# Opening of a transformer trunk written anew: modulation weights loaded ahead of tokens, their products as columns, tokens turned in pairs

## Chip, cores and metric

The kernel runs on one core of one Trainium2 chip. The time is the device time of an execution in microseconds (us); the profile shows one profiled execution with its own span.

## What is computed

A trunk of two layers over 1024 tokens of width 1024. Each layer scales and shifts an RMS norm by six vectors that come from the condition `c` through a matrix `w_mod`, projects it into three groups of attention heads (A, B, C), joins their outputs, and then does the same with a gated feed-forward part. The part that the change touches is the very first one, in layer 0:

```python
cond = jax.nn.silu(c)
mod = cond @ w_mod[l] + b_mod[l]                  # (1, 6 * 1024)
sh_a, sc_a, gt_a, sh_f, sc_f, gt_f = split_cols(mod, (D,) * 6)
h = rms_norm(x, g_attn[l]) * (1 + sc_a) + sh_a    # the opening computes this for l = 0
proj = h @ w_in[l]                                # ... and the first parts of this
```

All data are 32-bit. A value is kept as a high and a low part, so that a product takes three fast matmuls (high x high, low x high, high x low).

## The kernel before

TensorE is `pe`, ScalarE `act`, VectorE `dve`, GpSimd `pool`; SyncE (`sp`) issues nearly all loads, in order. Within the opening (lines 723 to 861) the order on `pe`, `act`, `dve` and `sp` is pinned as written: each engine does its instructions in the order of the program text. Only what comes after line 861 is ordered by the scheduler.

**Data.** Tokens come in two halves of 512, each as four tiles of 128 tokens (`x_load`, 512 KB each, in `xn`). A tile is squared and summed on ScalarE (`x_square`; its output `junk` is thrown away, the sum goes into a column of `rx`). `x_rms` takes the root and VectorE the reciprocal; `spread` turns these four columns into rows (`ps_r`, copied to `rb`). `x_turn` transposes the tokens on TensorE, four 128x128 blocks to a PSUM bank (`ps_x`), and copies them into `xt`, which holds the width on its partitions: block n of `xt` is the n-th 128 of the width.

**Modulation.** Only the shift and scale of the first norm are needed at once, 2048 of the 6144 columns. They are made in four pairs p; pair p serves blocks 2p and 2p + 1. A pair has two pieces of `w_mod`, i = 2p and 2p + 1, one for each half of the rows; `gm_load(i)` loads one in two transfers of 512 KB into one of three buffers (`gm`). `gemv_half(i)` handles a piece: VectorE multiplies three of its four 128-row parts by the condition and sums them into `ga`; the fourth goes to TensorE. With the second piece TensorE sums `ga` over its partitions (`ones`). In the kernel before this gives a row of 512 values in PSUM (`ps_mod`), which ScalarE copies (`gr`) and four small transposes bring onto partitions (`gemv_turn`, `ps_m`). `gemv_finish(p)` adds the bias and makes the scale `gsc`. The vectors for that (bias and gains, `v72`) are loaded by GpSimd and transposed by `turn_vecs`.

**The norm's output.** `h_blocks(half, rows, ns)` makes blocks of h: `nt` on VectorE (tokens x scale x rows), then the high part `hh` on ScalarE, then the low part `hl` on VectorE.

**First products.** `c_first(n)` multiplies block n with the first weights of group C for four token tiles into four PSUM banks (`pssC`): 12 matmuls of 512 columns. These weights come as four tiles of 512 KB (`wc_stage`), split in two parts by `w_high` (ScalarE) and the function that it returns (VectorE, `wlo`). `a_first(u, p)` does two of eight row blocks of one early tile of the A projection (`pssA`, two banks): 6 matmuls. Its weights (`a_stage`, `a_high`) lie in parts of `hh` and `hl` that the second tokens fill later. Weight tiles (of C, of A, and `wab`) go through two buffers of the tag `wst`. `keep_busy` issues matmuls whose results are not used.

**After the opening** the loop over t (line 1056) starts with `c_proj(4, 5)`, the projection of token tiles 4 and 5, which takes h of the second half block by block. `spill` writes `xt` to memory in the meantime.

Of the kernel before, what the change touches and what calls it, by code (L numbers as in the profile page):

```python
# [85 lines left out]
def trunk(ctx: ExitStack, tc, A, C, out):  # L86
# [479 lines left out]
    def x_square(half, j, xn, r):  # L566
        junk = xt[:, 6:8, half * H : (half + 1) * H]
        act.activation(
            junk, xn.rearrange("p (a b) -> p a b", a=2), AF.Square, accum_out=r[:, j : j + 1]
        )  # L570
# [5 lines left out]
    def x_turn(half, xn, ns, engines):  # L576

        c = slice(half * H, (half + 1) * H)
        for n in ns:
# [7 lines left out]
            else:  # L587
                dve.tensor_copy(xt[:, n, c], ps)

# [25 lines left out]
    def gemv_half(i):  # L615
        p, s = i // 2, i % 2
        gm = gms.pop(i).rearrange("p k g n -> p k (g n)")
        if s == 0:
            gas[p] = stp.tile([P, 4 * P], F32, name="ga", tag="ga", bufs=2)
            gps[p] = psl.tile([P, 4 * P], F32, name="ps_mod", tag="mm")  # L620
        ga, row = gas[p], gps[p][0:1]
        for k in range(3):
            mod_add(4 * s + k, ga, gm[:, k])
        pe.matmul(row, condT[:, 4 * s + 3 : 4 * s + 4], gm[:, 3], start=(s == 0), stop=False)
        if s:
            pe.matmul(row, ones, ga, start=False, stop=True)
            gas[p] = stp.tile([1, 4 * P], F32, name="gr", tag="gr", bufs=1)
            act.copy(gas[p], row)

    def gemv_turn(p):  # L630

        ps = gps[p] = psl.tile([P, 4], F32, name="ps_m", tag="mm")
        row = gas.pop(p)
        for c in range(4):
            pe.transpose(ps[:, c : c + 1], row[:, c * P : (c + 1) * P], ident[0:1, 0:1])
# [14 lines left out]
    def h_blocks(half, rows, ns):  # L650
# [11 lines left out]
        for n, t in ts.items():  # L662
# [3 lines left out]
            )  # L666

# [6 lines left out]
    def c_first(n):  # L674

        wh, wl = wC[n // 2]
        for t in range(T0):
            ts_ = slice(t * P, (t + 1) * P)
            mm3(
                pssC[t], hh[:, n, ts_], hl[:, n, ts_], wh[:, n % 2], wl[:, n % 2],  # L680
                n == 0, n == KC - 1,
            )
# [42 lines left out]
    sp.dma_start(c8, A["c"][0].rearrange("(k p) -> k p", p=P))  # L725
    xns = [[x_load(0, j) for j in range(4)], []]
# [3 lines left out]
    gm_load(0)  # L730
    gm_load(1)
    wc_stage(0)
    a_stage(0)
    gm_load(2)
    rxs = [stp2.tile([P, 4], F32, name="rx", tag="rx", bufs=2) for _ in range(2)]
    act.activation(c8, c8, AF.Silu)
    idle = psl.tile([P, 4, P], F32, name="ps_idle", tag="mm")
# [5 lines left out]

    pst = psl.tile([P, 512], F32, name="pst", tag="mm")
    pe.transpose(pst[:, :KC], c8, ident[:KC, :KC])
    dve.tensor_copy(condT, pst[:, :KC])
    keep_busy(18)
    for j in range(4):
        x_square(0, j, xns[0][j], rxs[0])
    x_rms(rxs[0])  # L750
    x_turn(0, xns[0], range(KC), (act, act))
    gemv_half(0)
# [1794 lines left out]
```

## Time and profile before

| | us |
|---|---|
| median of 3 runs | 2385.76 |
| lowest and highest | 2385.19, 2387.93 |
| the profiled execution | 2386.03 |
| its span, first to last instruction | 2384.3 |

A row of the timeline has the start, the duration, the engine, the operation, the tile written and those read, the shape, how many instructions were merged into it, and in brackets the idle time before it and what ended that. A wide matmul is listed with about 0.39 us; matmuls are pipelined, so the next one starts sooner than that. PEld is the load of TensorE's weights. A group of instructions has count, busy time and mean time of one in ns, then the idle time before them.

### The profile page before, as it was taken

The page shows a single profiled execution, that of the slowest core. Times are in us where ns is not written, and L with a number is a line of the kernel's source. Part 1 is how long each engine was busy: PE and PEld are TensorE (multiplying, and loading weights), DVE is VectorE, ACT ScalarE, POOL GpSimd, SP SyncE. Part 2 cuts the span into 40 slices and gives each one's busy share as a digit, 9 for nine tenths or more (in the row PEclk, how much of TensorE's full clock was granted, in tenths as well). Part 3 has the DMA queues.
Part 4 walks back from the last instruction along what each step waited for, and adds up shares of the span by engine and source line. Part 5 has one row for each costly group of instructions (what it writes and reads, how often), then busy time and mean ns, then how long its engine had stood idle before and what let it go on. Part 6 is the DMA issues. An engine that isn't in the chain of part 4 may idle for free. (4 is left out here: it accounts for less than half of the span.)

```text
span 2384.3 us, 33350 instructions
## 1 busy us (share of the span) xinstructions
PE 2330.1 (98%) x11733; PEld 1949.5 (82%) x11733; DVE 1757.3 (74%) x2754; ACT 1186.5 (50%) x2264; POOL 781.9 (33%) x747
## 2 busy tenths in 40 slices
PE   8999999999999999999999999999999999999998
PEld 5788898888788888788888889988888888888886
DVE  5777898967957687586777689987796664537765
ACT  4422788944543333344533158897454333334443
POOL 1441356810244444200135124575015443430001
PEclk9999999999999999999999999999999999999999
DMA  8567417164345444586434861242633443329743
GB/s 279 150 194 227 138 28 198 34 210 126 111 143 175 131 154 153 183 259 186 155 96 132 256 186 28 72 120 74 225 102 126 153 155 103 104 98 297 214 121 111
DMA packets 307416, 358.00 MB, mean 150 GB/s; under 512 B 51996, under 2 KB 223868, under 8 KB 307248
## 3 DMA queue, kind: packets, MB, share of 16 engines
q1 hardware_dynamic: 290752, 346.26, 46.6%
q10 hardware_dynamic: 16128, 9.44, 1.5%
q8 instruction: 92, 1.51, 0.3%
q14 instruction: 76, 0.62, 0.1%
q0 software_dynamic: 368, 0.17, 0.0%
HBM read 270.84 MB, written 88.63 MB: 151 GB/s over the span
## 5 line engine op out<-in xcount | busy, mean ns | idle before, releaser
L49 PE MATMUL ps_d<-wpt 128*128 128x512 f32 x1848 | 423.8, 390 | 1.0 <-ACT wpt L49 0.7
L49 PEld LDWEIGHTS ps_d<-wpt 128*128 128x128 f32 x1848 | 345.7, 188 | 74.4 <-issue 3.0
L49 POOL TENSOR_SCALAR pr<-pr,rs 128x1024 f32<-128x1024 f32 (+2 forms) x248 | 190.2, 781 | 188.7 <-DVE rs L49 171.1
L49 POOL TENSOR_TENSOR sg<-sg,u 128x512 f32<-128x512 f32 x82 | 126.8, 1548 | 347.1 <-ACT sg L49 221.6
L49 PE MATMUL pv<-pt,vs 128*128 128x256 f32 x1088 | 176.1, 296 | 16.3 <-DVE y L49 13.7
L49 ACT CAST wpt<-w 128x512 fp32r<-128x512 f32 x154 | 95.7, 621 | 175.7 <-PE ps_d L49 155.0
L49 DVE TENSOR_TENSOR pt<-T,pt 128x512 fp32r<-128x512 f32 x272 | 177.6, 680 | 7.0 <-ACT pt L49 5.9
L49 ACT CAST pt<-T 128x512 fp32r<-128x512 f32 x272 | 151.7, 586 | 42.4 <-PE T L49 40.7
L49 ACT COPY u<-ps_w 128x512 f32<-128x512 f32 x128 | 75.1, 586 | 192.0 <-PE ps_w L49 187.1
L49 DVE SCALAR_TENSOR_TENSOR acc<-wmt,condT,acc 128x512 f32<-128x512 f32 (+1 forms) x98 | 117.0, 1202 | 71.5 <-DMA wmt<-in_w_mod_dram 70.7
L49 DVE TENSOR_TENSOR wpt<-w,wpt 128x512 fp32r<-128x512 f32 x154 | 109.1, 708 | 79.7 <-ACT wpt L49 75.4
L49 POOL TENSOR_TENSOR wpt<-ws,wpt 128x512 fp32r<-128x512 f32 x80 | 110.7, 1384 | 171.2 <-ACT wpt L49 132.4
L49 PEld LDWEIGHTS pv<-pt,vs 128*128 128x128 f32 x1088 | 142.2, 189 | 29.7 <-DVE y L49 25.4
L49 PE MATMUL T<-identr,pr 128*128 128x128 f32 x1176 | 160.8, 273 | 0.8 <-ACT edge L49 0.4
L49 PEld LDWEIGHTS T<-identr,pr 128*128 128x128 f32 x1176 | 137.8, 140 | 15.5 <-ACT edge L49 1.1
L49 ACT CAST wpt<-ws 128x512 fp32r<-128x512 f32 x176 | 107.8, 622 | 51.4 <-issue 22.9
L49 DVE TENSOR_TENSOR wpt<-graw,wpt 128x512 fp32r<-128x512 f32 x154 | 110.2, 716 | 17.3 <-ACT wpt L49 17.3
L49 ACT CAST wpt<-graw 128x512 fp32r<-128x512 f32 x154 | 95.0, 617 | 51.7 <-DMA graw<-gpd 43.3
L49 DVE TENSOR_REDUCE rs<-sC 128x1 f32<-128x1024 f32 x88 | 107.2, 1220 | 12.5 <-PE sC L49 11.4
L49 DVE TENSOR_TENSOR wlo<-wst,whi 128x1024 fp32r<-128x1024 f32 (+1 forms) x70 | 91.6, 1313 | 33.3 <-ACT whi L49 29.4
L49 DVE TENSOR_TENSOR wpt<-ws,wpt 128x512 fp32r<-128x512 f32 x96 | 81.0, 852 | 47.5 <-ACT wpt L49 47.2
L49 DVE TENSOR_TENSOR ws<-wr 128x512 f32<-128x512 f32 x88 | 81.3, 924 | 46.5 <-POOL wpt L49 43.0
(308 smaller groups left out, 5966.1 us busy)
## 6 DMA issues: line engine op xcount, KB each, us to landing
wr<-in_w_gu_dram SPq DMA_DIRECT2D x92, 512.0 KB, 4.1
gpd<-sg SPq DMA_DIRECT2D x154, 256.0 KB, 4.4
graw<-gpd SPq DMA_DIRECT2D x76, 512.0 KB, 3.8
w<-in_w_down_dram SPq DMA_DIRECT2D x110, 256.0 KB, 5.0
wmt<-in_w_mod_dram SPq DMA_DIRECT2D x48, 512.0 KB, 5.7
qk<-qkd SPq DMA_DIRECT2D x44, 512.0 KB, 7.0
wst<-in_w_o_dram SPq DMA_DIRECT2D x32, 512.0 KB, 4.2
wmt<-in_w_mod_dram SPq DMA_DIRECT2D x64, 256.0 KB, 3.9
```

What stands on the lines that cost most here:

```text
L49: ins = op(*args, **kwargs)
```

## The change

- Loads: the first two pieces of `w_mod` are issued ahead of the token tiles; the second weight tile of C goes ahead of piece 4, the two early A tiles and the second half's tokens go to other places in the queue.
- `gemv_half` makes columns: a 128x128 block of the piece (or of `ga`) is the weight, one column of the condition (or of ones) is streamed, and the four results stand in four columns of a bank. The sum of `ga` is a function that it returns, called later. `gemv_turn` and the copy `gr` are gone. For pair 1 (`kd=2`) VectorE does two of four parts and TensorE two.
- `x_turn_first` turns two token tiles at a time: one bank holds two blocks of the width for two tiles, and its copies are returned as functions, to be issued on VectorE or ScalarE at a chosen place. The second half still goes through `x_turn`, all copies on ScalarE.
- The root's table is asked for at the start. The vectors are turned after the first pair's columns. `rb` has two buffers; the first `h_blocks` reads the spread rows from PSUM.
- `c_first` runs its 12 matmuls by pass and not by token tile, and can do some passes alone; `h_blocks` can issue something between its low parts.
- The order of all calls is new: blocks 2 to 5 of `c_first` and the modulation pieces alternate; squares, turns and `h_blocks` of the second tokens come earlier among them, and the first step of the head norm (`first`) too.

```diff
--- before.py
+++ after.py
@@ -564,7 +564,7 @@
         return t
 
     def x_square(half, j, xn, r):
-        junk = xt[:, 6:8, half * H : (half + 1) * H]
+        junk = xt[:, 6:8, H:S]
         act.activation(
             junk, xn.rearrange("p (a b) -> p a b", a=2), AF.Square, accum_out=r[:, j : j + 1]
         )
@@ -587,6 +587,22 @@
             else:
                 dve.tensor_copy(xt[:, n, c], ps)
 
+    def x_turn_first(xn, pair, ms):
+
+        c = slice(pair * 2 * P, (pair + 1) * 2 * P)
+        copies = []
+        for m in ms:
+            ps = psl.tile([P, 2, 2 * P], F32, name="ps_x", tag="mm")
+            for a in range(2):
+                n = 2 * m + a
+                for i in range(2):
+                    pe.transpose(
+                        ps[:, a, i * P : (i + 1) * P],
+                        xn[2 * pair + i][:, n * P : (n + 1) * P], ident,
+                    )
+            copies.append(lambda copy, m=m, ps=ps: copy(xt[:, 2 * m : 2 * m + 2, c], ps))
+        return copies
+
     def load_vecs(l):
         v = stp.tile([72, P], F32, name="v72", tag="v72", bufs=2)
         pool.dma_start(v[0:48], A["b_mod"][l].rearrange("(k p) -> k p", p=P))
@@ -612,27 +628,27 @@
             rows = A["w_mod"][0, r0 : r0 + 4 * P, c0 : c0 + 2 * P]
             sp.dma_start(gm[:, :, g, :], rows.rearrange("(k p) n -> p k n", p=P))
 
-    def gemv_half(i):
+    def gemv_half(i, kd=3):
         p, s = i // 2, i % 2
         gm = gms.pop(i).rearrange("p k g n -> p k (g n)")
         if s == 0:
             gas[p] = stp.tile([P, 4 * P], F32, name="ga", tag="ga", bufs=2)
-            gps[p] = psl.tile([P, 4 * P], F32, name="ps_mod", tag="mm")
-        ga, row = gas[p], gps[p][0:1]
-        for k in range(3):
+            gps[p] = psl.tile([P, 4], F32, name="ps_m", tag="mm")
+        ga, ps = gas[p], gps[p]
+        for k in range(kd):
             mod_add(4 * s + k, ga, gm[:, k])
-        pe.matmul(row, condT[:, 4 * s + 3 : 4 * s + 4], gm[:, 3], start=(s == 0), stop=False)
+
+        def columns(src, col, start, stop):
+            for c in range(4):
+                pe.matmul(
+                    ps[:, c : c + 1], src[:, c * P : (c + 1) * P], col,
+                    start=start and c == 0, stop=stop, skip_group_check=True,
+                )
+
+        for k in range(kd, 4):
+            columns(gm[:, k], condT[:, 4 * s + k : 4 * s + k + 1], s == 0 and k == kd, False)
         if s:
-            pe.matmul(row, ones, ga, start=False, stop=True)
-            gas[p] = stp.tile([1, 4 * P], F32, name="gr", tag="gr", bufs=1)
-            act.copy(gas[p], row)
-
-    def gemv_turn(p):
-
-        ps = gps[p] = psl.tile([P, 4], F32, name="ps_m", tag="mm")
-        row = gas.pop(p)
-        for c in range(4):
-            pe.transpose(ps[:, c : c + 1], row[:, c * P : (c + 1) * P], ident[0:1, 0:1])
+            return lambda: columns(gas.pop(p), ones, False, True)
 
     def gemv_finish(p):
 
@@ -647,7 +663,7 @@
             in1=vecs[0][:, 48 + 2 * p : 50 + 2 * p], op0=ALU.add, op1=ALU.mult,
         )
 
-    def h_blocks(half, rows, ns):
+    def h_blocks(half, rows, ns, between=None):
 
         c = slice(half * H, (half + 1) * H)
         ts = {}
@@ -664,6 +680,9 @@
                 out=hl[:, n, c], in0=t, scalar=mods[0][:, n : n + 1], in1=f32(hh[:, n, c]),
                 op0=ALU.add, op1=ALU.subtract,
             )
+            if between:
+                between()
+                between = None
 
     def wc_stage(kp):
         st = stage()
@@ -671,15 +690,17 @@
             sp.dma_start(dst, v)
         wcs.append(st)
 
-    def c_first(n):
+    def c_first(n, passes=range(3)):
 
         wh, wl = wC[n // 2]
-        for t in range(T0):
-            ts_ = slice(t * P, (t + 1) * P)
-            mm3(
-                pssC[t], hh[:, n, ts_], hl[:, n, ts_], wh[:, n % 2], wl[:, n % 2],
-                n == 0, n == KC - 1,
-            )
+        first, last = n == 0, n == KC - 1
+        for i in passes:
+            h, w = ((hh, wh), (hl, wh), (hh, wl))[i]
+            for t in range(T0):
+                pe.matmul(
+                    pssC[t], h[:, n, t * P : (t + 1) * P], w[:, n % 2],
+                    start=first and i == 0, stop=last and i == 2, skip_group_check=True,
+                )
 
     def a_stage(u):
         ast.append(w_ab(0, EARLY_AB[u]))
@@ -723,39 +744,23 @@
     pin((pe, act, dve, sp), True)
     c8 = stp.tile([KC, P], F32, name="c8")
     sp.dma_start(c8, A["c"][0].rearrange("(k p) -> k p", p=P))
+    gm_load(0)
+    gm_load(1)
     xns = [[x_load(0, j) for j in range(4)], []]
     v0, v1 = load_vecs(0), load_vecs(1)
     oneh = ccp.tile([32, 512], F32R, name="oneh")
     pool.dma_start(oneh, C["onehot"])
-    gm_load(0)
-    gm_load(1)
     wc_stage(0)
-    a_stage(0)
     gm_load(2)
     rxs = [stp2.tile([P, 4], F32, name="rx", tag="rx", bufs=2) for _ in range(2)]
     act.activation(c8, c8, AF.Silu)
+    act.activation(rxs[0][:, 0:1], epst, AF.Sqrt)
     idle = psl.tile([P, 4, P], F32, name="ps_idle", tag="mm")
 
     def keep_busy(n):
 
         for _ in range(n):
             pe.matmul(idle, identr, bc(identr[:, None, :], [P, 4, P]), start=True, stop=True)
-
-    pst = psl.tile([P, 512], F32, name="pst", tag="mm")
-    pe.transpose(pst[:, :KC], c8, ident[:KC, :KC])
-    dve.tensor_copy(condT, pst[:, :KC])
-    keep_busy(18)
-    for j in range(4):
-        x_square(0, j, xns[0][j], rxs[0])
-    x_rms(rxs[0])
-    x_turn(0, xns[0], range(KC), (act, act))
-    gemv_half(0)
-    gm_load(3)
-    ps = spread(rxs[0], 0, psl)
-    rb = stp2.tile([P, H], F32, name="rb")
-    act.copy(rb, ps)
-    turn_vecs(0, v0)
-    turn_vecs(1, v1)
 
     def w_high():
         st = wcs.pop(0)
@@ -764,86 +769,123 @@
         act.copy(hi, st)
         return lambda: sub(lo, st, f32(hi))
 
-    def w_split():
-        w_high()()
-
-    def pair_done(p):
-        gemv_turn(p)
-        gemv_finish(p)
-        if p == 0:
-            keep_busy(8)
-        h_blocks(0, rb, (2 * p, 2 * p + 1))
-
+    pst = psl.tile([P, 512], F32, name="pst", tag="mm")
+    pe.transpose(pst[:, :KC], c8, ident[:KC, :KC])
+    dve.tensor_copy(condT, pst[:, :KC])
+    keep_busy(10)
+    gemv_half(0)
+    gm_load(3)
+    wc_stage(1)
+    keep_busy(8)
+    x_square(0, 0, xns[0][0], rxs[0])
+    x_square(0, 1, xns[0][1], rxs[0])
+    columns = gemv_half(1)
+    gm_load(4)
     keep_busy(4)
-    lows = [w_high(), a_high(0)]
-    gemv_half(1)
-    gm_load(4)
-    xns[1].append(x_load(1, 0))
-    for low in lows:
-        low()
-    wc_stage(1)
-    keep_busy(2)
-    pair_done(0)
+    columns()
+    turn_vecs(0, v0)
+    turn_vecs(1, v1)
+    gemv_finish(0)
+    for copy in x_turn_first(xns[0], 0, range(4)):
+        copy(dve.tensor_copy)
+    x_square(0, 2, xns[0][2], rxs[0])
+    keep_busy(3)
+    x_square(0, 3, xns[0][3], rxs[0])
+    copies = x_turn_first(xns[0], 1, range(4))
+    copies[0](dve.tensor_copy)
+    x_rms(rxs[0])
+    rows = spread(rxs[0], 0, psl)
+    low = w_high()
+    copies[1](act.copy)
+    keep_busy(6)
+    h_blocks(0, rows, (0, 1), low)
+    a_stage(0)
+    for copy in copies[2:]:
+        copy(act.copy)
+    rb = stp2.tile([P, H], F32, name="rb", tag="rb", bufs=2)
+    act.copy(rb, rows)
     pssC = [psl.tile([P, 512], F32, name="ps_c", tag="mm") for _ in range(T0)]
+    c_first(0)
+    gemv_half(2, 2)
+    gm_load(5)
+    c_first(1, (0, 1))
+    low = w_high()
+    columns = gemv_half(3, 2)
+    gm_load(6)
+    columns()
+    c_first(1, (2,))
+    low()
+    wc_stage(2)
+    gemv_finish(1)
+    a_low = a_high(0)
+    for j in (0, 1):
+        xns[1].append(x_load(1, j))
+    h_blocks(0, rb, (2, 3))
+    c_first(2)
+    a_low()
     pssA = [psl.tile([P, 512], F32, name="ps_ab", tag="mm") for _ in range(2)]
-    gemv_half(2)
-    gm_load(5)
-    a_stage(1)
-    xns[1].append(x_load(1, 1))
-    c_first(0)
-    w_split()
-    wc_stage(2)
-    c_first(1)
-    gemv_half(3)
-    gm_load(6)
-    xns[1].append(x_load(1, 2))
     gemv_half(4)
     gm_load(7)
-    xns[1].append(x_load(1, 3))
     wc_stage(3)
-    pair_done(1)
-    a_high(1)()
+    for j in (2, 3):
+        xns[1].append(x_load(1, j))
+    c_first(3)
+    low = w_high()
+    columns = gemv_half(5)
+    low()
+    a_stage(1)
+    columns()
+    gemv_finish(2)
+    a_first(0, 0)
+    a_first(0, 1)
+    h_blocks(0, rb, (4, 5))
+    c_first(4)
     x_square(1, 0, xns[1][0], rxs[1])
-    a_first(0, 0)
-    c_first(2)
-    c_first(3)
-    w_split()
+    x_square(1, 1, xns[1][1], rxs[1])
+    gemv_half(6)
+    c_first(5)
+    low = w_high()
+    columns = gemv_half(7)
+    low()
     wab = [w_ab(0, 0)]
     g8 = gains_load(ccp, 0)
     t5 = ccp.tile([32, 6], F32, name="t5")
     sp.dma_start(t5, A["t5_table"])
-    gemv_half(5)
-    gemv_half(6)
-    pair_done(2)
-    x_square(1, 1, xns[1][1], rxs[1])
-    a_first(1, 0)
-    a_first(0, 1)
-    c_first(4)
-    c_first(5)
-    w_split()
-    wab.append(w_ab(0, 1))
-    spill(0)
-    gemv_half(7)
-    pair_done(3)
-    a_first(1, 1)
-    x_turn(1, xns[1], (0, 1), (dve, act))
-    a_first(0, 2)
     for j in (2, 3):
         x_square(1, j, xns[1][j], rxs[1])
     x_rms(rxs[1])
-    x_turn(1, xns[1], (2, 3), (dve, act))
+    columns()
+    gemv_finish(3)
+    x_turn(1, xns[1], (0,), (act, act))
+    a_low = a_high(1)
+    a_first(0, 2)
+    h_blocks(0, rb, (6, 7))
+    a_low()
+    wab.append(w_ab(0, 1))
+    spill(0)
+    rows = spread(rxs[1], 0, psl)
+    rb = stp2.tile([P, H], F32, name="rb", tag="rb", bufs=2)
+    act.copy(rb, rows)
+    x_turn(1, xns[1], (1,), (act, act))
     c_first(6)
-    x_turn(1, xns[1], (4, 5), (dve, act))
-    a_first(1, 2)
-    x_turn(1, xns[1], (6, 7), (dve, act))
-    rows = spread(rxs[1], 0, psl)
+    h_blocks(1, rb, (0, 1))
+    x_turn(1, xns[1], (2, 3), (act, act))
     c_first(7)
-    spill(1)
-    for u in (1, 0):
-        a_first(u, 3)
-    h_blocks(1, rows, (0, 1))
+    h_blocks(1, rb, (2, 3))
     gm = stp.tile([P, 2048], F32, name="gm", tag="gm", bufs=3)
     first = c_norm_first(pssC[0], gm[:, 0:512], gm[:, 512:1024], gm[:, 1024:1032])
+    a_first(1, 0)
+    a_first(1, 1)
+    x_turn(1, xns[1], (4, 5), (act, act))
+    next(first)
+    a_first(1, 2)
+    a_first(1, 3)
+    x_turn(1, xns[1], (6, 7), (act, act))
+    spill(1)
+    h_blocks(1, rb, (4, 5))
+    a_first(0, 3)
+    first_t1 = next(first)
+    h_blocks(1, rb, (6, 7))
 
     ra, ua = gm[0:8, 1032:1497], gm[0:8, 1500:2012]
     pool.dma_start(ra, A["rpb_na"].rearrange("l h i d -> (l h) (i d)"))
@@ -853,10 +895,6 @@
         ra.rearrange("p (e d) -> p d e", e=15),
     )
     pool.dma_start(skr, ua)
-    for n in range(2, KC, 2):
-        h_blocks(1, rows, (n, n + 1))
-        if n < 6:
-            first_t1 = next(first)
     sp.dma_start(sinkc, bc(A["sink_sw"].rearrange("l h -> (l h)")[None, :], [P, 12]))
     pin((pe, act, dve, sp), False)
     close(s2_cm)
```

## The prediction

> **What bounds the kernel now.** I read the page first, then the busy time by stretches, the waits of the matmul engine, the timeline of the opening, and the groups of instructions. Before the times stand the lines that they come from.
>
> ```profile
> span 2384.3 us, 33350 instructions
> PE 2330.1 (98%) x11733; PEld 1949.5 (82%) x11733; DVE 1757.3 (74%) x2754; ACT 1186.5 (50%) x2264; POOL 781.9 (33%) x747
> ...
> PE pv L49 <- DVE y L49: 13.7, 23, 1.3
> PE ps_w L49 <- ACT u L49: 3.3, 5, 0.8
> ...
> 4.00:48.00 44.00, 35.97 (x144) 22.27 (x143) 23.93 (x37) 20.45 (x32) 2.53 (x5) 0.92 1.06 350
> 48.00:60.00 12.00, 12.00 (x50) 7.49 (x49) 9.64 (x15) 3.95 (x6) 1.02 (x2) 1.00 0.23 65
> ...
> 32.00:36.00 4.00, 0.00 (x0) 0.00 (x0) 3.15 (x4) 0.74 (x1) 0.00 (x0) 0.61 1.09 329
> 36.00:40.00 4.00, 3.71 (x8) 0.55 (x8) 2.14 (x4) 0.57 (x1) 0.00 (x0) 0.54 0.90 302
> ...
> 36.29 1.87 PE L49 MATMUL ps_mod<-ga,onesr 128*1 128x512 f32 x2 [6.14 <-DVE ga L49]
> ...
> 80.82 0.39 PE L49 MATMUL ps_c<-whi,hh 128*128 128x512 f32 x1
> ```
>
> The columns of a stretch are PE, PEld, DVE, ACT and POOL busy, then clock, DMA share and GB/s. TensorE is busy for 98% of the span; its two longest waits after 100 us are short ones for VectorE and ScalarE, and none of its waits there is for a DMA. So what the opening saves on TensorE should be kept later. I take the opening to end where the projection of tokens 4 and 5 starts, at 80.82 us: from there TensorE has the same work in both kernels.
>
> The opening has two halves. From 4 to 48 us the DMA engines are full (share 1.06, 350 GB/s): 512 KB take 0.524 MB / 350 GB/s = 1.5 us. From 48 to 60 us they are nearly idle (65 GB/s), while TensorE goes on for 33 us to 80.82. The loads arrived in time to be used earlier; TensorE could not use them. The place is visible: nothing ran on it from 32 to 36 us, one wait was 6.14 us, and then the clock was 0.54. The same bytes are loaded after the change, so the question is how early TensorE gets its pieces in order.
>
> **The start of the first product.**
>
> ```profile
> 9.25 1.06 ACT L49 ACTIVATE xt<-xn 128x1024 f32<-128x1024 f32 x1 [0.49 <-DMA xn<-in_x_dram]
> 10.22 0.18 ACT L49 ACTIVATION_READ_ACCUMULATOR xt<-xn 128x1 f32 x1
> 10.42 1.28 ACT L49 ACT_TABLE_LOAD   x1
> 11.72 0.30 ACT L49 ACTIVATE rx<-rx,epst 128x4 f32<-128x4 f32 x1
> ...
> 12.05 0.18 DVE L49 RECIPROCAL rx<-rx 128x4 f32<-128x4 f32 x1 [8.56 <-ACT rx L49]
> ...
> 14.57 0.65 PE L49 MATMUL ps_r<-identr,rx 128*128 128x128 f32 x4
> ...
> 16.79 1.04 ACT L49 CAST whi<-wst 128x1024 fp32r<-128x1024 f32 x1 [0.40 <-DMA wst<-in_w_in_dram]
> ...
> 21.19 1.42 DVE L49 SCALAR_TENSOR_TENSOR nt<-xt,gsc,rb 128x512 f32<-128x512 f32 x2
> ...
> 21.98 1.39 ACT L49 ACTIVATE hh<-nt,mod 128x512 fp32r<-128x512 f32 x2 [1.89 <-DVE nt L49]
> ...
> 23.47 0.50 PE L49 MATMUL ps_c<-whi,hh 128*128 128x512 f32 x1
> ```
>
> In both orders the first projection weights are the ninth load of 512 KB; before they landed at 16.79. After, the last token tile is the eighth: 16.79 - 1.5 = 15.3, and I add 0.5 because the modulation pieces that now lead take longer to issue: 15.8 us (weights 17.3). From there: square 1.06 + 0.18, root 0.30 (its table is loaded while ScalarE waits for tokens, so the 1.28 us of 10.42 leave this chain), reciprocal 0.18, but VectorE first finishes five token copies, so 17.9; the spread over rows 0.65; one `nt` 0.71, one `hh` 0.70, hand-offs: the first product at 20.3 instead of 23.47. The modulation columns, which before came last here, are ready by then: four loads of 512 KB before the tokens, so about 9.8 us, then three VectorE passes and the last columns, about 13 us. The vectors are turned while TensorE waits for tokens, which hides them; without that cover they would cost well under 1 us. One risk: of eight PSUM banks four are still taken when the four accumulators are claimed. If one accumulator gets the bank of the last token tile, whose ScalarE copy comes after both `hh`, the start slips by up to 1.8 us. I take 0, for there are just four free.
>
> **TensorE's work from there.**
>
> ```profile
> L49 PE MATMUL ps_c<-whi,hh 128*128 128x512 f32 x32 | 12.9, 402 | 0.4 <-ACT hh L49 0.4
> ...
> L49 PE MATMUL ps_mod<-gm,condT 128*1 128x512 f32 x12 | 7.0, 669 | 0.0
> L49 PE MATMUL ps_ab<-hh 128*128 128x512 f32 x16 | 6.8, 423 | 0.0
> ...
> L49 PE MATMUL ps_mod<-ga,onesr 128*1 128x512 f32 x6 | 3.9, 740 | 6.1 <-DVE ga L49 6.1
> ...
> 24.27 0.40 PE L49 MATMUL ps_c<-whi,hh 128*128 128x512 f32 x1
> 24.50 0.39 PE L49 MATMUL ps_c<-whi,hl 128*128 128x512 f32 x1
> ...
> 10.04 3.66 PE L49 MATMUL ps_x<-identr,xn 128*128 128x128 f32 x32
> ...
> 13.62 1.02 PE L49 MATMUL ps_mod<-gm,condT 128*1 128x512 f32 x2
> ...
> 535.46 0.95 PE L49 MATMUL ps_st<-onesr,ssq 128*128 128x1 f32 x8
> ```
>
> Wide products follow each other by 24.50 - 24.27 = 0.23 us. `c_first` has 3 x 32 = 96 of them (21.8 us at 0.227), `a_first` 3 x 16 = 48 (10.9); 32 turns of second tokens take 3.7 and the spread 0.65. This stays. The modulation product changes form: before, a row of 512 columns took up to 0.74 us a pass and then went over ScalarE and four small transposes. Now a 128x128 block of weights meets one column. The same shape (128x128, 128x1, two passes a product) stands in the trace as `ps_st`: 8 passes in 0.95 us, 0.119 each. Pairs 1, 2 and 3 issue 20, 12 and 12 such products, 88 passes, 10.5 us. That is no saving against 18 row passes (7.0 + 3.9 us); what goes is the ScalarE copy and the transposes on the chain. The sum is 21.8 + 10.9 + 3.7 + 0.65 + 10.5 = 47.6 us: without any wait the opening would end at 20.3 + 47.6 = 67.9.
>
> **The walk, with the waits.**
>
> ```profile
> L49 DVE SCALAR_TENSOR_TENSOR ga<-gm,condT,ga 128x512 f32<-128x512 f32 x20 | 15.0, 750 | 0.6
> L49 DVE SCALAR_TENSOR_TENSOR hl<-nt,mod,hh 128x512 fp32r<-128x512 f32 x16 | 12.8, 836 | 0.9
> ...
> L49 DVE TENSOR_TENSOR wlo<-wst,whi 128x1024 fp32r<-128x1024 f32 x4 | 4.9, 1226 | 8.6 <-ACT whi L49 8.6
> ...
> 31.70 1.04 ACT L49 CAST whi<-wst 128x1024 fp32r<-128x1024 f32 x1 [8.34 <-DMA wst<-in_w_in_dram]
> ...
> 4.92 1.06 ACT L49 ACTIVATE xt<-xn 128x1024 f32<-128x1024 f32 x1 [2.47 <-DMA xn<-in_x_dram]
> ...
> 42.19 0.49 PE L49 MATMUL ps_c<-whi,hh 128*128 128x512 f32 x1 [0.41 <-ACT hh L49]
> ...
> 80.82:92.70 11.88, 11.49 (x49) 8.78 (x48) 11.43 (x16) 5.84 (x10) 4.77 (x4) 1.00 0.25 82
> ```
>
> Before, the second weight tile was queued behind modulation and token pieces and landed at 31.70; VectorE, in order, held the sums of pair 1 behind it (the 8.6 us), and block 2 started at 42.19. After, it is queued ahead of piece 4. At 1.5 us each: pieces 2 and 3 at 20.3 and 23.3, the weights 24.8, piece 4 27.8, early tile 29.3, pieces 5 and 6 32.3 and 35.3, weights 36.8, two token tiles 39.8, piece 7 42.8, weights 44.3, two token tiles 47.3, early tile 48.8.
>
> TensorE in its new order: block 0 20.3 to 23.2 (its third pass waits for `wlo`, which VectorE ends at 22.2), columns to 25.1, two thirds of block 1 to 26.9, columns and sum to 29.8, the rest to 30.7. The finish (two short VectorE steps), `nt` and `hh` give block 2 at 31.9: a wait of 1.2 us, and 10 us earlier than 42.19. Then block 2, columns, block 3 and columns to 40.3; two `a_first` parts to 43.0, which cover the next finish and `hh`; block 4 45.8, columns, block 5 49.4, columns 51.3; here VectorE has the sums of piece 7 and `wlo` behind it at 49, and the next `hh` comes at 54.2, as one turn, an `a_first` part, the spread and a second turn end. From 54.2 on tokens, weights and early tiles are all there: blocks 6 and 7, four `a_first` parts and the other turns, 15 us, to 69.2. I add six refills, each a first product of 0.50 in place of 0.23 us: 1.6. The forecast is the end of the opening at 70.8 instead of 80.82: 10.0 us sooner.
>
> Waits that are new: the early weight tile's load needs the buffer of the first weights, freed at 22.2; the rest of SyncE's queue (pieces 5 to 7, weights, tokens) stands behind it, but loads up to 27.8 are already queued, so it costs nothing with 5.6 us of cover. Pieces 5, 6 and 7 wait for TensorE's columns (25.1, 28.8, 36.5 with VectorE) while earlier loads last to 29.3, 32.3 and 39.8; the thinnest cover is 3.3 us. Second token copies go to ScalarE alone: 12 rather than 8 steps there, hidden beside 69 us with waits.
>
> VectorE ends the second `h` blocks at about 75.6 by the rows' durations; the last is needed when three quarters of tokens 4 and 5 are done, 70.8 + 8.2 = 79.0. So the cover is 3.4 us. That stretch had VectorE at 11.43 of 11.88, so it is close.
>
> **Rivals.**
>
> *The clock* (chance 0.10). Turns and one-column products may not keep it up. For: after an idle stretch it read 0.61 and 0.54. Against: 32 turns took 3.66 us, 0.114 each, and the two row passes right behind them 1.02, where cold ones took 1.87. If three stretches (after turns, after pair 1, after pair 3) ran 3.4 us of work at half speed, the cost is 3 x 1.7 = 5 us: 2381.
> The Trainium skill, "TensorE: Matmul & The Clock Gate", part 4, says that transposes do not count as PE-busy, which speaks against this change; the rows at 9 to 14 us do not show it. By that rule block 0 alone, after turns, would lose 2.7 us.
>
> *VectorE sets the pace* (0.10). In the opening `hl` took 836 ns on the mean; I walked with 0.71, half of the `nt` row. If 32 us of its work in the second half ran 15 to 25% longer, 5 to 8 us, less 3.4 of cover, cost 2 to 5: about 2379.
>
> *The gain is given back later* (0.08). If DVE, full beyond 80 us, or the order of the attention part took back all, 2385.8. Against: no TensorE wait there is for something with a time of its own.
>
> *The load queue runs dry* (0.12), the slower case. Now every later piece waits for TensorE, where before tokens filled between them. If the early tile's buffer came free over 5.6 us later than 22.2, the queue is empty, and each of pieces 5, 6 and 7 is loaded only after the columns that free its place: a load on an empty queue was used 4.92 - 1.21 = 3.7 us after its issue (the first token tile, issued at 1.21), and the piece's second half adds 1.5. That is 3 x 5.2 = 15.6 us: 86.4, 2391.4. Against: three covers of 3 us and more must go together.
>
> ```profile
> 1.21 1.79 SPq L49 DMA_DIRECT2D xn<-in_x_dram  x4
> ```
>
> **How the numbers follow.** The profiled execution took 2386.03 us, its span plus 1.7, and the median of the runs is 2385.76, 0.3 less; I take the difference of 10.0 off both: 2376.0 for the profiled one, 2375.8 for the median. The forecast has chance 0.60. Its own range: no wait at all (67.9) gives 2372.8, a start a little earlier 2372; the bank slip, one late load and doubled refills (1.8 + 1.5 + 1.6) give 2381. The range to 2384 takes in the clock and VectorE cases; outside lie the give-back and the dry queue, 0.20. A change of 0.2% is 4.8 us, about what a measurement of this kernel tells from none, so faster means under 2381.0. Faster: 0.60 + 0.06 of the clock + 0.09 of VectorE = 0.75. Same: 0.08 + 0.04 + 0.01 = 0.13. Slower: 0.12.
>
> **What would show it.** Right: first `ps_c` product near 20.3, block 2 near 32, no TensorE wait of 6 us and no clock under 0.9 after 16 us, DMA share about 1 to 47 us, the 96 + 48 wide products done near 71, `ps_m` passes of 0.12 us, the PE waits after 100 us as they are. Wrong: DMA share below 0.9 between 25 and 45 us (dry queue); products 0.43 us apart (clock); `ps_c` of tokens 4 and 5 waiting for `hl` (VectorE); or the opening ends at 71 and the span is not shorter (given back).

## The result and the profile after

The changed kernel takes 2376.33 us (median of 7 runs, 2375.63 to 2379.67) where the kernel before, run beside it, takes 2385.76 (7 runs, 2384.62 to 2387.93). The ratio is 0.9964, 95% interval 0.9954 to 0.9975. Three of the seven executions took 2378.89 to 2379.67 us with a mean granted clock of 0.995, the other four 2375.63 to 2376.33 with 0.996 to 0.998. The profiled execution took 2376.24 us. The forecast was 2375.8 with a range of 2372 to 2384.

The page's span and busy times, then the busy time by stretches (PE, PEld, DVE, ACT, POOL, then the granted clock, DMA share, GB/s), both of the changed kernel:

```profile
span 2374.4 us, 33475 instructions
...
PE 2327.5 (98%) x11804; PEld 1961.2 (83%) x11804; DVE 1754.3 (74%) x2753; ACT 1184.7 (50%) x2261; POOL 787.0 (33%) x747
```

```profile
4.00:48.00 44.00, 42.86 (x232) 36.29 (x230) 31.05 (x50) 18.44 (x29) 3.60 (x8) 0.92 1.04 346
...
12.00:16.00 4.00, 3.37 (x23) 3.19 (x23) 2.54 (x7) 3.50 (x7) 0.00 (x0) 0.79 1.02 397
16.00:20.00 4.00, 4.00 (x28) 3.74 (x27) 2.29 (x5) 2.93 (x5) 0.00 (x0) 0.79 1.09 351
...
28.00:32.00 4.00, 4.00 (x30) 3.72 (x29) 1.02 (x4) 1.06 (x1) 0.00 (x0) 0.92 0.98 299
32.00:36.00 4.00, 3.70 (x12) 2.47 (x11) 3.87 (x6) 1.39 (x2) 0.00 (x0) 0.65 1.05 330
36.00:40.00 4.00, 4.00 (x24) 3.43 (x23) 3.82 (x7) 1.05 (x1) 0.00 (x0) 1.00 0.97 341
```

The loads run as before: between 4 and 48 us the DMA share is 1.04 instead of 1.06. What changed is TensorE, busy for 42.86 of those 44 us instead of 35.97; the 4 us in which nothing ran on it are gone. But the clock is under 1.00 in two places: 0.79 around 16 us, 0.65 after 32. The timeline of TensorE shows what stands there:

```profile
12.81 1.05 PE L49 MATMUL ps_m<-onesr,ga 128*128 128x1 f32 x8 [0.63 <-DVE ga L49]
...
13.88 3.23 PE L49 MATMUL ps_x<-identr,xn 128*128 128x128 f32 x16
16.76 1.37 PE L49 MATMUL ps_idle<-identr 128*128 128x512 f32 x3
17.97 1.91 PE L49 MATMUL ps_x<-identr,xn 128*128 128x128 f32 x16
...
21.92 1.18 PE L49 MATMUL ps_c<-whi,hh 128*128 128x512 f32 x4 [0.20 <-ACT hh L49]
...
24.87 1.84 PE L49 MATMUL ps_m<-condT,gm 128*128 128x1 f32 x16
...
28.48 1.84 PE L49 MATMUL ps_m<-condT,gm 128*128 128x1 f32 x16
30.19 1.03 PE L49 MATMUL ps_m<-onesr,ga 128*128 128x1 f32 x8
31.08 1.83 PE L49 MATMUL ps_c<-wlo,hh 128*128 128x512 f32 x4
33.21 1.89 PE L49 MATMUL ps_c<-whi,hh 128*128 128x512 f32 x4 [0.30 <-ACT hh L49]
34.94 1.09 PE L49 MATMUL ps_c<-whi,hl 128*128 128x512 f32 x4
...
36.79 0.95 PE L49 MATMUL ps_m<-condT,gm 128*128 128x1 f32 x8
...
42.12 0.48 PE L49 MATMUL ps_ab<-hh 128*128 128x512 f32 x1
...
71.05 0.40 PE L49 MATMUL ps_c<-whi,hh 128*128 128x512 f32 x1
```

The first 16 turns (`ps_x`) took 3.23 us, the second 16 took 1.91. Four wide products take 1.07 to 1.19 us, but 1.83 and 1.89 around 33 us: half rate. The first product starts at 21.92 (before 23.47), block 2 at 33.21 (before 42.19), and the opening ends at 71.05 (before 80.82). That is 9.77 us sooner, and 9.0 of it stand already at block 2. The span shrank by 9.9, the profiled execution by 9.79.

The waits of TensorE after 100 us are nearly those of before, but the one for `own` has grown from 0.4 to 1.7 us:

```profile
PE pv L49 <- DVE y L49: 13.8, 23, 1.3
...
PE ps_ab L49 <- DVE own L49: 1.7, 1, 1.7
```

### The profile page after: what moved, and what is told of

The parts are those of the page before. It is cut to its first block, busy times and chain, and to the rows that moved or that the text cites. A ratio compares the mean times of both kernels' runs of the same rounds, so it can differ in the third digit from the quotient of the medians.

```text
span 2374.4 us, 33475 instructions
## 1 busy us (share of the span) xinstructions
PE 2327.5 (98%) x11804; PEld 1961.2 (83%) x11804; DVE 1754.3 (74%) x2753; ACT 1184.7 (50%) x2261; POOL 787.0 (33%) x747
## 5 line engine op out<-in xcount | busy, mean ns | idle before, releaser
L49 DVE TENSOR_TENSOR wpt<-graw,wpt 128x512 fp32r<-128x512 f32 x154 | 110.2, 715 | 17.3 <-ACT wpt L49 17.3
L49 DVE TENSOR_REDUCE rs<-sC 128x1 f32<-128x1024 f32 x88 | 107.2, 1220 | 12.6 <-PE sC L49 11.6
L49 PE MATMUL ps_w<-ht3h,wpt 128*128 128x512 f32 x352 | 108.9, 391 | 2.5 <-ACT sg L49 2.5
```

Of the source, the lines that this page charges most:

```text
L49: ins = op(*args, **kwargs)
```

## The experiments

All times are medians of 5 to 11 runs; the ratio to the kernel before has its 95% interval. The last four columns are read from one profiled execution of each.

| kernel | median us | ratio | first product | block 2 | opening ends | wait for `own` |
|---|---|---|---|---|---|---|
| before | 2385.76 | | 23.47 | 42.19 | 80.82 | 0.4 |
| changed | 2376.33 | 0.9964 [0.9954, 0.9975] | 21.92 | 33.21 | 71.05 | 1.7 |
| changed, again | 2377.14 | 0.9964 [0.9951, 0.9976] | 21.67 | 32.98 | 71.59 | 1.7 |
| 1 rows | 2378.42 | 0.9968 [0.9957, 0.9980] | 22.16 | 34.84 | 75.10 | none |
| 2 tokens first | 2385.84 | 0.9993 [0.9984, 1.0001] | 30.32 | 42.01 | 81.01 | 1.7 |
| 3 tokens first, busy | 2382.58 | 0.9983 [0.9974, 0.9992] | 25.57 | 36.90 | 76.73 | 1.7 |
| 4 weights late | 2381.60 | 0.9983 [0.9974, 0.9992] | 23.61 | 37.72 | 75.95 | 1.7 |
| 5 before, pair 1 first | 2384.91 | 0.9998 [0.9989, 1.0007] | 24.23 | 36.48 | 79.77 | 0.4 |
| 6 before, all pairs first | 2383.46 | 0.9992 [0.9983, 1.0001] | 24.02 | 36.28 | 79.32 | 0.4 |
| 7 busier | 2377.04 | 0.9961 [0.9948, 0.9973] | 20.96 | 32.29 | 72.18 | 1.7 |
| 8 three on VectorE | 2375.88 | 0.9954 [0.9940, 0.9968] | 23.76 | 33.71 | 72.46 | 1.7 |
| 9 both | 2375.59 | 0.9956 [0.9944, 0.9969] | 20.95 | 31.58 | 71.53 | 1.7 |
| 10 both, and busy ahead of block 2 | 2372.78 | 0.9946 [0.9933, 0.9960] | 20.66 | 32.34 | 69.51 | none |
| 11 busier, and busy ahead of block 2 | 2373.98 | 0.9950 [0.9936, 0.9963] | 20.88 | 33.38 | 71.07 | none |

**1. The products as rows again, everything else as in the change.** Is it the columns or the order?

```diff
-            columns(gm[:, k], condT[:, 4 * s + k : 4 * s + k + 1], s == 0 and k == kd, False)
...
+            pe.matmul(
+                row, condT[:, 4 * s + k : 4 * s + k + 1], gm[:, k],
+                start=(s == 0 and k == kd), stop=False,
+            )
...
+            act.copy(gr, row)
...
+                pe.transpose(ps[:, c : c + 1], gr[:, c * P : (c + 1) * P], ident[0:1, 0:1])
```

> The changed kernel with the modulation product as a row again (row of 512, ScalarE copy, four small transposes), in the new order of work. Theory 'order' (the new order of loads and work gives the gain, the form of the product is incidental): pair 1 costs TensorE about as much (10 row passes of 0.43 us and the transposes against 40 of 0.12), the finish of each pair is 1.3 us later, which is hidden for pairs 0 and 3, and the two clock dips of the changed kernel (12 to 20 and 28 to 36 us), which follow one-column passes, go: 2375.5 to 2378.5. Theory 'form' (the shorter chain without ScalarE is the gain): most of the 9.4 us is lost, 2382 or more.

The opening ends 4.05 us later, and the waits that the columns remove are back:

```profile
PE ps_m L49 <- ACT gr L49: 3.0, 4, 0.9
```

The clock is 1.00 in every stretch from 8 to 44 us here. The median lies only 2.1 us above the changed kernel's; 1.8 us of the 4.05 are made up by 385 us, and that is about the size of the wait for `own`, which this kernel lacks. So the rest of the change, with rows, carries 5.7 of the 9.8 us, and the columns bring some 4 in the opening.

**2. The tokens loaded first, as before.** Only `gm_load(0)` and `gm_load(1)` go back behind the four `x_load`.

```diff
-    gm_load(0)
-    gm_load(1)
     xns = [[x_load(0, j) for j in range(4)], []]
...
     pool.dma_start(oneh, C["onehot"])
+    gm_load(0)
+    gm_load(1)
```

> The changed kernel with the first four token tiles issued ahead of the first two modulation pieces, as before; the order on the engines stays. The sums of piece 1 then end near 18 us and the first product starts near 26.5 instead of 21.9. Theory 'TensorE paces from its first product on' (no slack behind it): the end of the opening moves by the same 4.6 us, about 2381. Theory 'loads pace the middle' (a late start is absorbed in waits that end with loads of 35 to 50 us): under 1.5 us is lost, 2376.5 to 2378.

```profile
8.00:12.00 4.00, 0.58 (x4) 0.52 (x4) 0.00 (x0) 2.36 (x5) 0.00 (x0) 0.97 1.10 337
12.00:16.00 4.00, 3.22 (x10) 2.74 (x11) 2.17 (x4) 0.00 (x0) 0.00 (x0) 0.50 1.08 358
...
PE ps_m L49 <- DMA gm<-in_w_mod_dram: 4.5, 2, 3.3
...
20.62 1.70 PE L49 MATMUL ps_m<-onesr,ga 128*128 128x1 f32 x8
...
22.46 3.38 PE L49 MATMUL ps_x<-identr,xn 128*128 128x128 f32 x16
25.59 0.94 PE L49 MATMUL ps_idle<-identr 128*128 128x512 f32 x3
```

By the median the whole gain is gone, twice what was expected. TensorE waits for the pieces, and then runs at a clock of 0.50 from 12 to 24 us: eight one-column passes take 1.70 us instead of 0.95, 16 turns 3.38. The first product slips by 8.4 us and, with a second stretch at 0.50 (40 to 44 us), the end by 10.0: what is lost ahead of the first product comes out at the end. But the eleven executions spread from 2381.12 to 2387.32 us, and the profiled one is the longest of them; five, at 2381.12 to 2383.37, are near the 2381 of the expectation.

**3. The same with more unused matmuls**, to part the wait from the clock: `keep_busy(10)` becomes 32 and the one ahead of the first `columns()` becomes 7.

> Tokens ahead of modulation as in the run before of that kind, and in addition matmuls whose results are not used while TensorE waits for pieces 0 and 1 (32 instead of 10 ahead of piece 0, 7 instead of 4 ahead of the first sum). Without them TensorE stood idle from 8 to 12 us, its clock read 0.50 from 12 to 24 us and the first product came at 30.3. Theory 'clock' (about half of that loss was the halved clock, the load order alone costs 4 to 5 us): clock 1.00 to 28 us, first product at 26 to 27, end of the opening near 76, 2379.5 to 2382. Rival 'load order alone': first product at 29 or later, 2384 or more.

The clock is 1.00 up to 32 us and the end 4.3 us earlier. So of the 10 us of that profile about 4.3 were the early clock. The other 5.7 are mostly the late pieces; a later dip, longer than the changed kernel's, remains in them (0.50 and 0.67 from 36 to 44 us).

**4. The second weights late.** In the change they are queued ahead of piece 4; here they trade places with the early tile and come behind it, and their low part is again made ahead of the sums of piece 3. The split of the early tile (`a_high(0)`, not shown) moves ahead of block 0 with its load.

```diff
     gm_load(3)
-    wc_stage(1)
+    a_stage(0)
...
     h_blocks(0, rows, (0, 1), low)
-    a_stage(0)
+    wc_stage(1)
...
-    low = w_high()
+    w_high()()
     columns = gemv_half(3, 2)
```

> The changed kernel with the second weight tile and the early tile exchanged in the load queue, and the low part of the second weight tile ahead of the sums of piece 3 on VectorE, both as before. The weights land near 30.2, the low part ends near 32.4, the sums near 34, block 2 starts near 37 instead of 33.2. Theory 'order on VectorE and the weight load' (this place made the 6 us wait before): 3.8 us are lost and go through to the end, about 2380. Rival (the wait before was of loads in general and is absorbed): under 1 us, 2376 to 2377.5.

```profile
PE ps_m L49 <- DVE ga L49: 2.6, 2, 1.8
```

Block 2 slips by 4.5 us and the end by 4.9: TensorE waits for sums that stand behind the weight split, as before the change, and the clock falls to 0.50 after it. But 1.7 us of this stand already at the first product (23.61), ahead of the weights: the clock was 0.59 and 0.56 from 12 to 20 us, a deeper first dip than in the changed kernel's profile. From the first product on the edit costs 3.2 us, where 3.8 were expected. The median of eleven runs is 5.3 us higher.

**5. The kernel before, with pair 1 finished ahead of the second weights' split.** One part of the new order alone.

```diff
     c_first(0)
-    w_split()
-    wc_stage(2)
     c_first(1)
     gemv_half(3)
     gm_load(6)
     xns[1].append(x_load(1, 2))
+    pair_done(1)
+    w_split()
+    wc_stage(2)
     gemv_half(4)
```

> The kernel before with one edit: pair 1 is finished (sums of piece 3, row, h blocks 2 and 3) ahead of the split of the second weight tile and of piece 4; loads ahead of it, tokens first and rows stay as before. Theory 'order' (9 of the 9.8 us were gained between the first product and block 2, by VectorE's and TensorE's order alone): block 2 near 33 to 35 instead of 42.2, no idle stretch of 6 us, clock not halved at 32 to 40, the end of the opening 71.5 to 74, 2377 to 2380. Rival 'the parts work together' (without columns and the new loads the next load sets the time): 2383 or more.

Block 2 comes 5.7 us earlier, but 1.05 are left at the end:

```profile
43.10 1.04 ACT L49 CAST whi<-wst 128x1024 fp32r<-128x1024 f32 x1 [4.67 <-DMA wst<-in_w_in_dram]
44.18 1.23 DVE L49 TENSOR_TENSOR wlo<-wst,whi 128x1024 fp32r<-128x1024 f32 x1 [3.38 <-ACT whi L49]
...
47.70 1.87 PE L49 MATMUL ps_mod<-ga,onesr 128*1 128x512 f32 x2 [3.71 <-DVE ga L49]
```

The same knot one pair later: the third weights land at 43.10, VectorE holds the sums of piece 5 behind their split, and TensorE waits 3.7 us for them.

**6. The kernel before, with every later pair finished ahead of its weight split** (the same edit at pairs 2 and 3).

> The kernel before with all three later pairs finished ahead of the split of the next weight tile (the run of this kind moved only pair 1 and met the same wait at the next weights: TensorE 3.7 us for the sums of piece 5, which stood behind weights that landed at 43.1). Theory 'VectorE's queue: sums behind a split that waits for a load': that wait goes, end of the opening 75 to 77 instead of 79.8, 2379 to 2381.5. Rival 'rows and tokens first set the time': 2383 or more.

The wait for `ga` is down to 1.0 us, yet the end gains only 1.5 us and the median about 2, with an interval that reaches 1. So finishing the pairs first is not enough in the old opening: TensorE still waits for the rows' copies (2.8 us for `gr`) and for weights that land late (2.6 us for `whi` and `wlo`).

**7. Five more unused matmuls ahead of the first turns,** against the first clock dip: `keep_busy(4)` becomes 7, and `keep_busy(2)` stands ahead of `gemv_finish(0)`.

> The changed kernel with five more unused matmuls (7 instead of 4 ahead of the first sum, 2 ahead of the first turns), to hold the clock that fell to 0.79 at 12 to 20 us. Theory 'clock': the first 16 turns take 1.9 us instead of 3.2, the first product comes near 20.5 instead of 21.9, and since nothing behind it waits for loads the end moves by as much: 69.6, 2374.5 to 2375.5. Rival 'the last token tile sets the first product' (it landed at 15.9 and its chain takes 4.5 us): under 0.5 us, 2376 to 2376.6.

The first dip is gone (1.00 to 28 us, the first product at 20.96). But the second grew (0.92, 0.50, 0.72 from 28 to 40 us), and the end came 1.1 us later than the changed kernel's. The expectation missed: the first product came 1.0 us sooner, where 1.4 were expected, and the later dip took more than that back.

**8. Pair 1 with three of four parts on VectorE,** as the other pairs: 24 one-column passes stand ahead of block 2 instead of 40.

```diff
-    gemv_half(2, 2)
+    gemv_half(2)
...
-    columns = gemv_half(3, 2)
+    columns = gemv_half(3)
```

> The changed kernel with pair 1 split like the others (three parts on VectorE, one on TensorE): 16 one-column passes fewer (1.9 us of TensorE), two VectorE sums more (1.5 us). Theory 'one-column passes do not keep the clock' (40 of them from 24.9 to 31.1 us came right before a clock of 0.65): no dip at 28 to 36 us, the first passes of block 2 0.23 apart instead of 0.45, block 2 near 32 instead of 33.2, end near 69.8, 2374.5 to 2375.5. Rival 'VectorE then sets pair 1': the last sum waits, block 2 not earlier than 33, 2376 to 2378.

```profile
33.71 2.08 PE L49 MATMUL ps_c<-whi,hh 128*128 128x512 f32 x4 [0.95 <-ACT hh L49]
```

From the first product to block 2 it takes 10.0 us instead of 11.3. The first dip was deeper in this execution (0.65, 0.50; first product 23.76), with the same instructions up to there as in the change. The second dip did not go, against the expectation: the clock is 0.71 and 0.86 from 32 to 40 us, behind 0.95 us of idle time. So fewer one-column passes alone did not keep the clock.

**9. Both.**

> Both edits together, the more unused matmuls and the split of pair 1 three to one. Theory 'clock': both dips gone, first product near 20.5, block 2 near 30.5, end of the opening near 68.4, 2373 to 2374.5, the best of all, and the runs closer together than those of the changed kernel (2375.6 to 2379.7), since the clock no longer differs between executions. Rival: one of the waits for loads comes up (piece 5 or 7, or the weights at 36.8 and 44.3) and keeps the end at 70 to 71, 2375.5 to 2377.

```profile
31.58 2.07 PE L49 MATMUL ps_c<-whi,hh 128*128 128x512 f32 x4 [1.63 <-ACT hh L49]
```

Block 2 is the earliest of all, but TensorE stood still for 1.63 us ahead of it, and its four products then took 2.07 us: half rate (0.50 from 32 to 36 us). The opening ends at 71.53, so the expectation of no dips and an end near 68.4 missed.

**10. Both, and six unused matmuls right ahead of that wait.**

```diff
     c_first(1, (2,))
+    keep_busy(6)
     low()
```

> The run with both edits (more unused matmuls early, pair 1 split three to one) and six unused matmuls right before block 2, where TensorE stood 1.6 us for the high part and the clock then read 0.50 from 32 to 36 us. Theory 'clock: an idle microsecond between one-column passes is enough to halve it for a window': no dip from 28 to 40 us, the passes of blocks 2 0.23 apart, the end of the opening near 69 instead of 71.5, median 2372.5 to 2374 where the run without them had 2375.6. Rival 'the loads keep the end' or 'the unused matmuls stand in the way': 2375 or more.

```profile
20.66 1.19 PE L49 MATMUL ps_c<-whi,hh 128*128 128x512 f32 x4 [0.20 <-ACT hh L49]
...
32.34 1.19 PE L49 MATMUL ps_c<-whi,hh 128*128 128x512 f32 x4 [1.31 <-ACT hh L49]
...
69.51 0.40 PE L49 MATMUL ps_c<-whi,hh 128*128 128x512 f32 x1
...
78.41 0.50 PE L49 MATMUL ps_c<-whi,hl 128*128 128x512 f32 x1 [0.32 <-DVE hl L49]
...
79.55 0.50 PE L49 MATMUL ps_c<-whi,hl 128*128 128x512 f32 x1 [0.18 <-DVE hl L49]
```

```profile
32.00:36.00 4.00, 3.66 (x20) 3.15 (x21) 3.65 (x5) 0.90 (x2) 0.00 (x0) 1.00 1.09 368
```

The clock is 1.00 in every stretch. 2372.78 us is the lowest median here, 3.6 below the changed kernel and 4.4 below its second run; the intervals of the ratios (0.9933 to 0.9960, 0.9954 to 0.9975) just overlap. The profile does not account for all of it: its execution took 2375.36 us, 0.9 less than the changed kernel's. Its opening ends 1.5 us sooner and the wait for `own` (1.7) is absent, but by 381 us it is only 1.4 us ahead. Part of what was gained is lost right behind the opening, where TensorE now waits 0.5 us for `hl`.

**The changed kernel again,** beside 6 and 10.

> The changed kernel itself once more, beside the others on the same chip: 2375.6 to 2379.7 as before, median near 2376.5; a second profile shows whether its two clock dips (0.79 at 12 to 20, 0.65 at 32 to 36) stand at the same place. If the dips depend on the phase of the clock's own window, the first product and block 2 move by 1 to 2 us between the two profiles.

It keeps its time. Its granted clock dips only at the second place, but the timeline shows a slow stretch earlier:

```profile
12.00:16.00 4.00, 4.00 (x31) 3.68 (x31) 0.98 (x6) 3.82 (x7) 0.00 (x0) 1.00 1.02 399
...
32.00:36.00 4.00, 3.04 (x8) 2.44 (x8) 3.84 (x7) 1.39 (x2) 0.00 (x0) 0.60 1.05 324
```

```profile
7.47 1.70 PE L49 MATMUL ps_m<-condT,gm 128*128 128x1 f32 x8
9.04 3.60 PE L49 MATMUL ps_idle<-identr 128*128 128x512 f32 x8
```

The eight unused matmuls took 2.08 us in the first profile. Here they ran at half rate, although the clock reads 1.00 there; so the column does not show the slow start of an execution (the ten unused matmuls ahead of them took 3.85 to 4.63 us in every profile with `keep_busy(10)`, where 0.23 us each would be 2.3). The first turns then run at full rate but begin at 15.28 instead of 13.88, and the first product comes at 21.67, 0.25 sooner than in the first profile. Block 2 moves by 0.23, less than the 1 to 2 us expected.

**11. Experiment 7 with the six unused matmuls of 10,** so that 40 one-column passes stand ahead of block 2, and unused matmuls where TensorE would stand idle.

> The changed kernel with 5 more unused matmuls ahead of the first turns and 6 more ahead of block 2, but pair 1 as in the change (two of four parts on VectorE, 40 one-column passes ahead of block 2 where the last version has 24). If the second clock dip came from TensorE standing idle before block 2, the 6 matmuls cure it here too: clock 1.00 throughout, block 2 at about 32.5, the opening ends at 69.5 to 70, median 2372.5 to 2374.5. If it came from the one-column passes themselves, the clock is still below 0.9 somewhere between 28 and 40 us, the opening ends at 71 to 72.5 and the median is 2375.5 to 2377.5.

```profile
27.45 1.84 PE L49 MATMUL ps_m<-condT,gm 128*128 128x1 f32 x16
29.15 1.03 PE L49 MATMUL ps_m<-onesr,ga 128*128 128x1 f32 x8
30.04 1.18 PE L49 MATMUL ps_c<-wlo,hh 128*128 128x512 f32 x4
31.06 2.52 PE L49 MATMUL ps_idle<-identr 128*128 128x512 f32 x6
33.38 1.72 PE L49 MATMUL ps_c<-whi,hh 128*128 128x512 f32 x4
```

```profile
28.00:32.00 4.00, 4.00 (x27) 3.69 (x27) 1.99 (x5) 1.20 (x2) 0.00 (x0) 0.92 1.10 337
32.00:36.00 4.00, 4.00 (x13) 3.14 (x13) 3.48 (x6) 1.08 (x2) 0.00 (x0) 0.66 1.08 363
```

TensorE is busy for 4.00 of 4.00 us and the clock falls all the same, right behind the passes: six unused matmuls took 2.52 us, 1.53 in experiment 10. The dip and the end at 71.07 are as the theory of the passes has them, in one profiled execution. The median is not: it is 2.35 us below the changed kernel's at the same end of the opening. By 382 us this kernel is 2.0 us ahead, and 1.7 of that is the wait for `own` that it does not have.

## Why the prediction was right, and where not

**The bound and the main term held.** TensorE could not use loads that were already there; the weight split ahead of the sums held it up. Experiments 4, 5 and 6 show that knot from both sides. Block 2 came 8.98 us sooner (10 were walked), no load queue ran dry, and the gain passed through: at the product that stands at 392 us before, the changed kernel is 9.97 us ahead, and at the end of the profiled execution 9.79. But the parts don't add: the tokens' place, the second weights' place and the columns cost 10.0, 4.9 and 4.05 us at the opening's end when each alone is undone (4.3 of the first and 1.7 of the second by the early clock), and finishing the pairs first brings 1 to 1.5 in the old opening. So each part seems to need the others; no run adds them one by one.

**The first product: 20.3 predicted, 21.92 measured.** ScalarE and VectorE show where the chain lost its 1.6 us:

```profile
15.95 1.06 ACT L49 ACTIVATE xt<-xn 128x1024 f32<-128x1024 f32 x1
...
17.14 0.30 ACT L49 ACTIVATE rx<-rx,epst 128x4 f32<-128x4 f32 x1
17.34 1.03 ACT L49 CAST whi<-wst 128x1024 fp32r<-128x1024 f32 x1
...
18.61 0.69 DVE L49 COPY xt<-ps_x 128x512 f32<-128x512 f32 x1 [0.77 <-PE ps_x L49]
19.22 0.17 DVE L49 RECIPROCAL rx<-rx 128x4 f32<-128x4 f32 x1
```

The loads were as walked: the last token at 15.95 (15.8), the weights by 17.34 (17.3), the root at 17.14. The reciprocal, at 19.22, was to come at 17.9: VectorE's fifth copy stood ahead of it and waited for turns, and the first 16 turns took 3.23 us instead of 16 x 0.114 = 1.8. The step that failed is that VectorE finishes its five token copies by 17.9, and its cause is the half rate of TensorE: during the turns in this profile, ahead of them in the kernel's second one. With the clock kept up the first product came at 20.66 to 20.96 in experiments 7, 9, 10 and 11.

**The walk held, the refills were too dear.** From the first product to block 2 it took 11.3 us (11.6 walked). Behind block 2 the dip cost the four products 1.73 us instead of 0.9. From the `a_first` parts to the end it took 71.05 - 42.12 = 28.9 us, the 28.9 walked from 40.3 to 69.2, which leaves nothing for the 1.6 us of six refills. A first product behind turns or passes costs 0.1 us and not 0.27: the next one starts after 0.32 instead of 0.23 (69.58 and 69.90). The one-column passes, cheaper than walked, gave part of that back. So that the forecast end, 70.8, was near 71.05 is in part luck: a term that was too large (1.6) and a start that the clock made late (1.6) had the same size. Experiment 10, without dips and with somewhat different work, ends at 69.51: the walk without refills said 69.2.

**The one-column pass** was priced a little too high. Eight are listed with 0.95 us at full clock, as in the row of before, but what follows them starts 0.81 us after the first (36.79 to 37.60): 0.10 us a pass, not 0.119.

**The rivals.** *The clock* came true in part: two dips instead of three, some 2.4 us instead of 5, and 4.3 us in experiment 2. In the changed kernel most of the turns behind one-column passes ran at half rate, while in experiment 11 turns behind unused wide matmuls ran at 1.91 us per 16. The Trainium skill, "TensorE: Matmul & The Clock Gate", part 4, says that transposes do not count as busy. The trace of experiment 2 does not agree: its clock was at 0.50 to 25 us, one-column passes and then turns were all that ran from 20.62 on, and the unused matmuls right behind the turns, at 25.59, ran at full rate (three in 0.94 us). Part 1 of that page of the Trainium skill lets the clock fall after about 3.4 us without work; the measurement differs here, for in experiment 11 it fell with no idle time at all. *VectorE's pace* cost nothing that the changed kernel's waits show, but its cover was thinner than walked: its second `h` blocks end at 78.85 us, not 75.6, and in experiment 10 TensorE waits 0.5 us for them. *Given back later*: "the PE waits after 100 us as they are" was wrong by one line, 1.7 us for `own`; other waits made it up by 392 us. *The dry queue*: from 4 to 48 us the DMA share stayed at 0.97 or more. In the second profile it was 0.81 from 36 to 40 us, and TensorE waited for no load.

**Left open.** Why the first dip comes in one execution and not in the next of the same instructions (0.79 in one profile of the changed kernel, 1.00 in the other). The traces show what goes with it: read in half-microsecond stretches, the clock of an execution changes only at the ends of equal stretches of 3.41 us, and these lie elsewhere in each execution (last section). A stretch that holds mostly one-column passes in one execution can end among wide products in the next. That this decides is argued, not tried. And the wait for `own`: it is 1.7 us in each kernel with the columns, except the two where the unused matmuls' tile is in use up to block 2, 0.4 in each kernel with the old opening, and none with rows in the new order. So it goes with the program, not with the execution. That fits a PSUM bank handed on around the ring of eight: the accumulator of the A projection would get the bank from which VectorE still reads. This too is argued, not tried. The feed-forward stretch of layer 0 (535 to 1173 us in the kernel before) takes 635.3 to 638.9 us in the profiled executions, with no visible relation to the edits; that is why differences of medians under about 2 us are not read here.

## What to carry to other kernels

When the loads run full and the matmul engine still stands idle, look for the in-order engine that holds a ready step behind one that waits for a load; then move the load, the step and its consumers together, since in experiments 5 and 6 the moved step alone soon met the next wait. Price a new kind of matmul twice, by the time from its start to the next start and by what it does to the clock for the wide products behind it, and try unused wide matmuls with a trace: the same six held the clock behind 24 one-column passes and not behind 40. A sum that comes out right is checked term by term: here a term that was too large and a missing one had the same size.

## What the hardware showed beyond the forecast

- Forty one-column passes with twelve wide products among them, in 7 us (experiment 11), brought the clock from 1.00 to 0.50 at 31.3 us without any idle time. Twenty-four of them with six unused wide matmuls and then 1.31 us of idle time (experiment 10) did not. The same 24 without the six matmuls, with 0.95 us (experiment 8) or 1.63 us (experiment 9) of idle time, did. Each is one profiled execution. At half rate four wide products took 1.7 to 2.1 us instead of 1.1.
- The clock stayed at 0.50 for 3.41 us or a multiple of it: 3.42 and 3.41 in the changed kernel, 6.83 before, 13.65 in experiment 2. Two falls in one execution lie a whole multiple apart, within a few hundredths: 14.28 and 31.35 (17.07, 5 x 3.41) in the changed kernel, 13.24 and 33.72 (20.48, 6 x 3.41) in experiment 8, 11.80 and 39.10 (27.30, 8 x 3.41) in experiment 2. So each such stretch can cost up to 1.7 us of full-rate work.
- An idle stretch of 3.34 us (experiment 2) was followed by a clock of 0.50 from 11.8 to 25.45 us. One-column passes, twelve unused wide matmuls and turns filled this time; that the wide ones were too few to raise the clock sooner is a reading, not tried by itself.
